# Grouped attention values, joined gate and up rows, and moved split and router steps in a hybrid encoder layer

## The chip, the cores and the metric

One core of one Trainium2 chip runs the whole layer as one program. The metric is device time in microseconds; the median of three runs before the change is 1883.89 us (1882.89 to 1885.06). The engines are named as the profile names them: PE multiplies matrices (PEld loads its weights), DVE, ACT and POOL do elementwise work, SP issues most transfers.

## What is computed

The layer mixes tokens (Fourier, neighbourhood attention and memory attention, gated and projected by `w_out`), normalises, and then sends each of 1024 tokens to 2 of 64 experts.

```python
proj = x @ w_in                                   # Fourier | q k v of the neighbourhood | memory q
br_na  = neighbourhood_attention(q_na, k_na, v_na, rpb) @ w_na_o
merged = gates[0] * br_f + gates[1] * br_na + gates[2] * br_mem
h = layer_norm(ALPHA * x + merged @ w_out)
# hierarchical_moe(h): one group of 8 by argmax, then the top 2 experts in it
yb = (jax.nn.silu(xb @ w_eg[e]) * (xb @ w_eu[e])) @ w_ed[e]
x = layer_norm(ALPHA * h + moe)
```

Everything is float32. An expert has a gate and an up matrix (1024 x 512 each) and a down matrix (512 x 1024), 2 MB apiece: 6.3 MB for each expert, 403 MB for all 64. An expert's tokens fill 64 slots.

## The kernel before

The first half (class `Dense`) is a chain of stages: the Fourier branch, neighbourhood attention (`na`), memory attention (`mem_attn`), `merge`, and the output projection with the router (`out_proj`). Large products are made in three products of rounded halves (a high and a low part made by `split`, L150: ACT copies, DVE subtracts). The input projections and gates are "jobs" of 48 matmuls of 128x512 each (L201); `adv(n)` puts n of them between the steps of the attention stages, so that PE always has something to do. A planner orders each engine's instructions by a simulated timeline; `keep_in_program_order` (also called `pin`) fixes the place of an instruction among the pinned ones of its engine.

**Neighbourhood attention.** Work goes by units (head pair `hp`, column block `j`, half of the rows `hf`, head of the pair `a`): `scores`, softmax, then one unit later `turned` (three transposes, L583). After the last of the four units of one (hp, j), `values` (L586, L593) issues eight products. Each is float32, which the trace shows as two matmul instructions, so a call is 16 instructions and there are 16 calls. Products for head a = 0 write the partitions 0 to 63 of a bank and those for a = 1 the partitions 64 to 127, and the program issues them in turn: a = 0, a = 1. They are not pinned.

**Merge.** For d = 0 to 7 two products of 24 matmuls each (L167) are made from weights that come through the raw tile `gr` (three buffers) and are split into `gh` and `gl`. In d = 1 to 4 `halves` (L710) sends two of the eight parts of `w_out` through the same three buffers: four transfers and four splits for each d. `w_out`'s halves stand in four 16 KB tiles `blk` of the pool WO.

**Output projection.** Eight tiles of 128 tokens, 48 matmuls each (L931), all pinned. Between the matmuls, at the places that the table `AT` (L783) lists, stand steps of earlier tiles: "t" transposes, "l" logits, "p" and "b" the middle and last part of `Moe.route`. "p" (L1132, L1133) counts with a table M that DVE has just made (L1126). `sums` (L807, L811) is put into the first tile once. `more()` issues the next weight transfer from SP: at tiles 0, 1, 2, 3 and 7, two more in `after(7)`, and then two from POOL behind the last tile (L1669).

**Experts.** `load` (L1324) brings 192 blocks of 2 MB (gate, up, down) into nine 16 KB-wide tiles: three in B1, two in Mg, four in WO; Mg and WO come free when `merge`'s and `out_proj`'s data have been used. A row, that is the bytes of one partition in one transfer, has 16 KB; the last expert is sent in four pieces a block (4 KB rows). For each expert `up` issues 8 pairs of products (gate to partitions 0 to 63, L1293; up to 64 to 127, L1294), `down` 4 pairs (L1315, L1316). `ahead` issues as many further loads as buffers come free. The transfers' waits for a free buffer stand on SP.

Of the kernel before, what the change touches and what calls it, by code (L numbers as in the profile page):

```python
# [5 lines left out]
F32 = mybir.dt.float32  # L6
FR = mybir.dt.float32r
# [8 lines left out]
D = 1024  # L16
T = 1024
NK = D // 128
# [110 lines left out]
class Dense:  # L129
# [116 lines left out]
    def start(s, pool):  # L246
# [22 lines left out]
        for j in range(2):  # L269
            s.wt[j] = [pool.tile([128, NK, 128], FR, name=n, bufs=2) for n in ("wh", "wl")]  # L270

# [273 lines left out]
    def na(s, fill):  # L545
# [39 lines left out]

        def values(u):  # L586
            hp, j, _, _ = u
            K = 4 * KCOLS[s.ORDER[j]][1]
            if j % 2 == 0:
                s.po = s.bank("o")  # L590
            for g, i, c in ((1, 1, slice(0, 2)), (0, 0, slice(0, 1)), (3, 0, slice(1, 2)), (2, 2, slice(0, 2))):
                for a in range(2):
                    nc.tensor.matmul(s.po[64 * a:64 * a + 64, j % 2 * 256 + c.start * 128:j % 2 * 256 + c.stop * 128],  # L593
                                     s.V[:K, j, g, hp * 128 + 64 * a:hp * 128 + 64 * a + 64],
                                     pts[a][:K, i, c].rearrange("p h f -> p (h f)"), start=g == 1, stop=g == 2)
            if j == 1:
# [10 lines left out]
        units = [(hp, j, hf, a) for hp in range(4) for j in range(4) for hf in range(2) for a in range(2)]  # L607
        old = None
        for i in range(len(units) + 1):
            u = units[i] if i < len(units) else None  # L610
            if u and u[1:] == (0, 0, 0):
                hp = u[0]
                if hp == 0:
                    s.finish("v3")
                s.finish(f"q{hp}")
                s.finish(f"k{hp}")
                s.adv(16)
                if hp == 0:
                    biases(0, "m")
                biases(hp, "e")  # L620
            if u and u[1:] == (2, 0, 0) and u[0] < 3:
                biases(u[0] + 1, "m")
            if u:
                sc = scores(u)
            s.adv(fill // 2)
            if old:
                turned(*old)
                s.adv(fill - fill // 2)
                if old[0][2:] == (1, 1):
                    values(old[0])  # L630
            old = (u, sc)

# [63 lines left out]
    def merge(s, W, pool, On, WO):  # L696
# [57 lines left out]

        blk = lambda: WO.tile([128, 4 * D], F32, name="blk", bufs=4)
        t = blk()
        raw = [t[:, k * D:(k + 1) * D] for k in range(4)]
# [6 lines left out]
        for d in range(8):  # L764
            get("s1", d, s.g_dram[8:])
            if d < 7:
                weights(0, d + 1)
                mem(d + 1)
                parts(0, d + 1)
            if d < 6:  # L770
                weights(1, d + 2)
                parts(1, d + 2)
            for k in range(2 * d - 2, 2 * d) if 0 < d < 5 else ():
                if k % 4 == 0:
                    s.wo.append([blk().bitcast(FR) for _ in range(2)])
                c = slice(k % 4 * D, (k % 4 + 1) * D)
                halves(*(t[:, c] for t in s.wo[-1]), A["w_out"][:, k])
            product(0, d)
            add_na(d)
        ps.release()  # L780


    AT = ((((11, "t", 1), (17, "l", 1)), ((11, "t", 0), (14, "p", 1), (17, "l", 0), (22, "b", 1))),  # L783
          (((11, "t", 1), (17, "l", 1)), ((21, "t", 0), (22, "p", 1)), ((6, "l", 0), (12, "t", 0), (16, "b", 1), (21, "l", 0))))

    def out_proj(s, P, P0, ps, lg, h_dram, done, more):
# [60 lines left out]
        def after(t, pl):  # L847
# [13 lines left out]
            if t == 7:  # L861
                for _ in range(2):
                    more()
            d = nc.gpsimd.dma_start(h_dram[t * 128:(t + 1) * 128], xts[t])
# [187 lines left out]
def moe_layout(i):  # L1052
    a = {}
    for n, k in (("w_exp_gate", 8), ("w_exp_up", 8), ("w_exp_down", 4)):
        w = np.asarray(i[n])[0]
        a[n] = np.ascontiguousarray(w.reshape(NE, k, 128, w.shape[2]).transpose(0, 2, 1, 3)).reshape(NE, 128, 4096)
    r = np.arange(128)
# [16 lines left out]
class Moe:  # L1074
# [210 lines left out]

    def up(s, ws, xT, mp, ps, nb, pin=lambda i: i):

        nc = s.nc
        wg, wu = ([w.rearrange("p (k f) -> p k f", f=512)[:, k] for w in ws[i] for k in range(w.shape[1] // 512)] for i in range(2))
        pg = ps.tile([128, 512], F32, name="pg")  # L1290
# [18 lines left out]

    def down(s, ws, hT, ps, bank="pd", pin=lambda i: i):  # L1310
        nc = s.nc
        wd = [w.rearrange("p (k f) -> p k f", f=1024)[:, k] for w in ws[2] for k in range(w.shape[1] // 1024)]
        pd = ps.tile([128, 512], F32, name=bank)
# [10 lines left out]
    def load(s, i, pool, bufs, eng=None):  # L1324

        e, k = s.ORDER[i]
        w = pool.tile([128, 4096], F32, name="blk", bufs=bufs)
        m = 1 if i < 3 * NE - 3 else 4
        for j in range(m):
            c = slice(j * 4096 // m, (j + 1) * 4096 // m)  # L1330
            d = (eng or s.nc.sync).dma_start(w[:, c], s.A[("w_exp_gate", "w_exp_up", "w_exp_down")[k]][e, :, c])
        return w, d

    def experts(s, w, more):
# [138 lines left out]

        def weights(e, k):
            return [w[s.ORDER.index((e, k))]]

        def up(e):
            c = slice(e % 2 * 64, e % 2 * 64 + 64)
            return s.up([weights(e, k) for k in range(2)], [xts[e // 2, i][:, j, c] for i in range(2) for j in range(4)], mp, ps, 1, pin)

        def ahead(n):
            while len(w) < min(3 * NE, n):
                d = more()
                if len(w) > 3 * NE - 6:
                    pin(d)

        for e in range(NE + 1):
# [3 lines left out]
            if e < NE:  # L1493
                gu = up(e)
                ahead(3 * e + 10)
            if e == 0:
# [10 lines left out]
            if e and e != NE - 1:  # L1507
                if e == NE:
                    last = half(FR)[:, :GR], mp.tile([128, 512], FR, name="gu"), half(FR)
                pd = s.down([None, None, weights(e - 1, 2)], hT, ps, "pd" if e < NE else "pg", pin)  # L1510
                ahead(3 * e + 11)
                new = accumulate(e - 1, pd)
# [15 lines left out]
            if e == NE - 2:  # L1528
                add(*accumulate(e, s.down([None, None, weights(e, 2)], hT, ps, pin=pin)))
        ps.release()  # L1530
# [3 lines left out]
    def slow(s, norm):  # L1534
# [5 lines left out]
        with tc.If(n > 0):  # L1540
# [15 lines left out]
            with tc.For_i(0, n, 1):  # L1556
# [21 lines left out]
                with tc.For_i(0, NE, 1) as e:  # L1578
                    c = nc.values_load(remi[0:1, bass.ds(e, 1)], min_val=-16 * SL, max_val=T)
                    with tc.If(c > 0):  # L1580
# [6 lines left out]
                        ws = []  # L1587
                        for nm in ("w_exp_gate", "w_exp_up", "w_exp_down"):
                            w = mp.tile([128, 4096], F32, name="o" + nm)
                            nc.sync.dma_start(w, A[nm][bass.ds(e, 1)].rearrange("o p f -> (o p) f"))  # L1590
                            ws.append([w])
                        pd = s.down(ws, s.act(s.up(ws, s.transposed(xg, mp, ps, 1), mp, ps, 1), mp, ps, 1), ps)
                        y = mp.tile([128, 512], F32, name="oy")
# [40 lines left out]
def build(tc, A):  # L1634
# [23 lines left out]

    pools = [(B1, 3)] * 3 + [(d.Mg, 2)] * 2 + [(d.WO, 4)] * 4

    def more(eng=None):
        i = len(w)
        t, ins = m.load(i, *pools[i % len(pools)], eng=eng)
        w.append(t)
        return ins
    d.out_proj(P, P0, ps, m.lg, h_dram, route, more)
    m.indices(P, *tabs)
    for _ in range(2):
        tc.keep_in_program_order(more(nc.gpsimd))  # L1669
    m.fetch(0)  # L1670
# [28 lines left out]
```

## Time and profile before

| | us |
|---|---|
| median of 3 runs | 1883.89 |
| the profiled execution | 1888.03 |
| its span, first to last instruction | 1886.3 |
| dense stages, to the last matmul of the output projection | 908 |
| experts, from there | 978 |

A profile comes from one execution. Where the rows give times such as 399.71, they are microseconds from the span's start. A matmul's record is longer than the distance to the next one, since matmuls overlap in the array; so what a matmul costs is read here from the start of one to the start of the next.

### The profile page before, as it was taken

To read this page: it belongs to the slowest core of one execution; us is meant where nothing else is said; L and a number is where in the kernel's file an instruction comes from. 1 tells how busy PE (TensorE), PEld (TensorE's weight loads), DVE (VectorE), ACT (ScalarE), POOL (GpSimd) and SP (SyncE) were. 2 spreads that over 40 slices of the span, in tenths; PEclk is the share of its full clock that TensorE was granted. 3 is DMA by queue.
4 is the path that set the end of the run, shared out by engine and by line. 5 is a ranking of instruction groups with operands and counts; after the bars stand their busy time and mean duration, and the time that the engine had idled before them with its cause. 6 is when DMAs were issued, how large, how long until landed. Compare 5 with 4: busy or idle time off the path is not lost. (4 is left out here: it accounts for less than half of the span.)

```text
span 1886.3 us, 23170 instructions
## 1 busy us (share of the span) xinstructions
PE 1819.5 (96%) x9290; PEld 1116.2 (59%) x9291; DVE 678.4 (36%) x1610; ACT 445.8 (24%) x819; POOL 126.5 (7%) x108
## 2 busy tenths in 40 slices
PE   8999999999999999999899999999999999999995
PEld 6988888777777777777644444434343343344331
DVE  5343234453442537677612222112221121212212
ACT  4332123343333432111211212112120121111211
POOL 1000100101200000000100101001010010100100
PEclk9999999999999999999999999999999999999998
DMA  7254513323233237652799999999999999999993
GB/s 280 71 196 152 195 45 98 99 95 110 93 95 128 79 140 248 217 201 101 306 411 426 427 426 427 428 418 427 426 426 428 426 427 425 422 427 427 427 426 156
DMA packets 77991, 527.31 MB, mean 280 GB/s; under 512 B 10447, under 2 KB 12383, under 8 KB 53176
## 3 DMA queue, kind: packets, MB, share of 16 engines
q1 hardware_dynamic: 55448, 469.31, 61.1%
q10 hardware_dynamic: 16352, 35.07, 5.5%
q0 software_dynamic: 6080, 21.42, 3.0%
q8 instruction: 74, 1.21, 0.3%
q14 instruction: 37, 0.30, 0.1%
HBM read 493.59 MB, written 32.51 MB: 279 GB/s over the span
## 5 line engine op out<-in xcount | busy, mean ns | idle before, releaser
L1294 PE MATMUL pg<-blk,xT 128*64 128x512 f32 x1024 | 456.6, 599 | 24.2 <-DMA blk<-in_w_exp_up 24.1
L1293 PE MATMUL pg<-blk,xT 128*64 128x512 f32 x1024 | 464.2, 601 | 0.3 <-ACT xT L1383 0.3
L1416 DVE SCALAR_TENSOR_TENSOR yl<-pd,wcol,yh 128x512 fp32r<-128x512 f32 x63 | 47.3, 751 | 667.7 <-ACT yh L1415 667.7
L201 PE MATMUL mm<-xl,wh 128*128 128x512 f32 x672 | 266.2, 396 | 0.0
L201 PE MATMUL mm<-xh,wh 128*128 128x512 f32 x672 | 265.1, 394 | 0.0
L201 PE MATMUL mm<-xh,wl 128*128 128x512 f32 x672 | 264.3, 394 | 0.0
L1294 PEld LDWEIGHTS pg<-blk,xT 128*64 128x64 f32 x1024 | 135.7, 137 | 202.5 <-issue 146.2
L1316 PE MATMUL pd<-blk,hTe 128*64 128x512 f32 x504 | 226.6, 592 | 0.0
L1315 PE MATMUL pd<-blk,hTe 128*64 128x512 f32 x504 | 226.6, 592 | 0.0
L1293 PEld LDWEIGHTS pg<-blk,xT 128*64 128x64 f32 x1024 | 132.7, 137 | 139.0 <-issue 134.7
L1296 ACT ACTIVATE gu<-pg 128x512 f32<-128x512 f32 x64 | 38.2, 597 | 567.1 <-PE pg L1294 567.1
L201 PEld LDWEIGHTS mm<-xh,wh 128*128 128x128 f32 x672 | 126.4, 188 | 25.5 <-issue 0.9
L201 PEld LDWEIGHTS mm<-xl,wh 128*128 128x128 f32 x672 | 126.4, 188 | 25.3 <-issue 1.6
L201 PEld LDWEIGHTS mm<-xh,wl 128*128 128x128 f32 x672 | 126.4, 188 | 25.0 <-issue 0.9
L1316 PEld LDWEIGHTS pd<-blk,hTe 128*64 128x64 f32 x504 | 69.0, 137 | 82.8 <-issue 82.8
L1315 PEld LDWEIGHTS pd<-blk,hTe 128*64 128x64 f32 x504 | 69.0, 137 | 61.2 <-issue 60.8
L152 DVE TENSOR_TENSOR wl<-wr,wh 128x1024 fp32r<-128x1024 f32 (+2 forms) x54 | 64.3, 1193 | 112.7 <-ACT wh L151 112.2
L1415 ACT ACTIVATE yh<-pd,wcol 128x512 fp32r<-128x512 f32 x63 | 43.3, 687 | 176.6 <-PE pd L1316 176.6
L151 ACT ACTIVATE wh<-wr 128x1024 fp32r<-128x1024 f32 (+2 forms) x54 | 55.5, 1028 | 109.0 <-PE mm L201 105.7
L931 PE MATMUL mm<-blk,mh 128*128 128x512 f32 (+1 forms) x272 | 70.9, 394 | 0.8 <-ACT mh L151 0.8
L1368 PE MATMUL tp<-sel,hh 128*128 128x128 f32 x248 | 70.1, 283 | 0.8 <-DVE xT L1371 0.8
L1369 PE MATMUL tp<-sel,hl 128*128 128x128 f32 x248 | 68.2, 275 | 0.0
(371 smaller groups left out, 2451.7 us busy)
## 6 DMA issues: line engine op xcount, KB each, us to landing
blk<-in_w_exp_up SPq DMA_DIRECT2D x63, 2048.0 KB, 37.0
blk<-in_w_exp_gate SPq DMA_DIRECT2D x62, 2048.0 KB, 32.9
blk<-in_w_exp_down SPq DMA_DIRECT2D x62, 2048.0 KB, 39.1
wr<-in_w_g SPq DMA_DIRECT2D x24, 512.0 KB, 3.7
g_dram<-gt ACTq DMA_DIRECT2D x48, 256.0 KB, 2.1
s<-g_dram SPq DMA_DIRECT2D x32, 256.0 KB, 3.9
be<-in_rpb_e ACTq DMA_DIRECT2D x8, 576.0 KB, 5.8
gt<-g_dram SPq DMA_DIRECT2D x8, 512.0 KB, 4.6
```

What stands on the lines that cost most here:

```text
L151: s.nc.scalar.activation(hi, src, AF.Copy)
L152: s.nc.vector.tensor_tensor(out=lo, in0=src, in1=hi.bitcast(F32), op=OP.subtract)
L201: s.nc.tensor.matmul(p[:, :width], st[:, k], x[:, k, c], start=k == 0 and pi == 0, stop=k == NK - 1 and pi == 2)
L931: pin(nc.tensor.matmul(p, (mh, mh, ml)[i][:, k], wo[c.start // 512][i % 2][:, at:at + w], start=j == 0, stop=j == m - 1))
L1293: pin(nc.tensor.matmul(pg[0:64], l, wg[k], start=k == 0, stop=k == 7))
L1294: pin(nc.tensor.matmul(pg[64:128], l, wu[k], start=k == 0, stop=k == 7))
L1315: pin(nc.tensor.matmul(pd[0:64], hT[:, f], wd[f][:, 0:512], start=f == 0, stop=f == 3))
L1316: pin(nc.tensor.matmul(pd[64:128], hT[:, f], wd[f][:, 512:1024], start=f == 0, stop=f == 3))
L1368: pin(nc.tensor.matmul(tp[:, j], hh[:, c], o[:, 0], start=True, stop=False))
L1369: pin(nc.tensor.matmul(tp[:, j], hl[:, c], o[:, 0], start=False, stop=False))
L1415: nc.scalar.activation(yh, pd, AF.Copy, scale=s.wcol[:, e:e + 1])
L1416: nc.vector.scalar_tensor_tensor(yl, pd, s.wcol[:, e:e + 1], yh.bitcast(F32), op0=OP.mult, op1=OP.subtract)
```

## The change

- `values` is pinned, and a call is issued one unit later: behind the scores of the next unit but one, ahead of the next `turned`.
- Gate and up of an expert are interleaved on the host into one array, and come in one transfer of 4 MB with rows of 32 KB. B1, WO and Mg hold the same bytes, now as three 32 KB tiles for gate and up and three 16 KB tiles for down. `w_out`'s high and low halves share one 32 KB tile.
- `more()` is called at tiles 0, 1, 3 and 7, once in `after(7)` and once from POOL.
- `halves` sends one part of `w_out` in each of d = 0 to 7.
- In `AT`, "p" goes from place 14 to 18 and "b" from place 22 of the tile to place 3 of the next one; `sums` goes from place 10 to 19.
- At the start the split weights of the second job go to the pool W.

```diff
-            s.wt[j] = [pool.tile([128, NK, 128], FR, name=n, bufs=2) for n in ("wh", "wl")]
+            s.wt[j] = [(pool, s.W)[j].tile([128, NK, 128], FR, name=n, bufs=1 + j) for n in ("wh", "wl")]
...
-        def values(u):
+        def values(u, pts):
...
-                    nc.tensor.matmul(s.po[64 * a:64 * a + 64, j % 2 * 256 + c.start * 128:j % 2 * 256 + c.stop * 128],
-                                     s.V[:K, j, g, hp * 128 + 64 * a:hp * 128 + 64 * a + 64],
-                                     pts[a][:K, i, c].rearrange("p h f -> p (h f)"), start=g == 1, stop=g == 2)
+                    s.tc.keep_in_program_order(nc.tensor.matmul(
+                        s.po[64 * a:64 * a + 64, j % 2 * 256 + c.start * 128:j % 2 * 256 + c.stop * 128],
+                        s.V[:K, j, g, hp * 128 + 64 * a:hp * 128 + 64 * a + 64],
+                        pts[a][:K, i, c].rearrange("p h f -> p (h f)"), start=g == 1, stop=g == 2))
...
             s.adv(fill // 2)
+            if due:
+                values(*due)
+                due = ()
             if old:
                 turned(*old)
                 s.adv(fill - fill // 2)
                 if old[0][2:] == (1, 1):
-                    values(old[0])
-            old = (u, sc)
+                    due = old[0], dict(pts)
+            old = (u, sc) if u else None
...
-            for k in range(2 * d - 2, 2 * d) if 0 < d < 5 else ():
-                if k % 4 == 0:
-                    s.wo.append([blk().bitcast(FR) for _ in range(2)])
-                c = slice(k % 4 * D, (k % 4 + 1) * D)
-                halves(*(t[:, c] for t in s.wo[-1]), A["w_out"][:, k])
+            if d % 4 == 0:
+                t = blk().bitcast(FR)
+                s.wo.append([t[:, :4 * D], t[:, 4 * D:]])
+            c = slice(d % 4 * D, (d % 4 + 1) * D)
+            halves(*(t[:, c] for t in s.wo[-1]), A["w_out"][:, d])
...
-    AT = ((((11, "t", 1), (17, "l", 1)), ((11, "t", 0), (14, "p", 1), (17, "l", 0), (22, "b", 1))),
-          (((11, "t", 1), (17, "l", 1)), ((21, "t", 0), (22, "p", 1)), ((6, "l", 0), (12, "t", 0), (16, "b", 1), (21, "l", 0))))
+    AT = ((((3, "b", 2), (11, "t", 1), (17, "l", 1)), ((11, "t", 0), (17, "l", 0), (18, "p", 1))),
+          (((3, "b", 2), (11, "t", 1), (17, "l", 1)), ((21, "t", 0), (22, "p", 1)), ((6, "l", 0), (12, "t", 0), (16, "b", 1), (21, "l", 0))))
...
-            if t in (0, 1, 2, 3, 7):
+            if t in (0, 1, 3, 7):
...
-                    if (t, n, j) == (0, 1, 10):
+                    if (t, n, j) == (0, 1, 19):
...
-    ORDER = [(e - k // 2, k) for e in range(NE - 1) for k in range(3) if 0 <= e - k // 2]
-    ORDER += [(NE - 2, 2)] + [(NE - 1, k) for k in range(3)]
+    ORDER = [("gu", 0), ("d", 0), ("d", 1), ("d", 2), ("gu", 1), ("gu", 2), ("gu", 3)]
+    ORDER += [x for e in range(4, NE - 1) for x in (("gu", e), ("d", e - 1))] + [("d", NE - 2), ("gu", NE - 1), ("d", NE - 1)]
...
                 gu = up(e)
-                ahead(3 * e + 10)
+                if e < NE - 4:
+                    upto("gu", e + 3)
...
-    pools = [(B1, 3)] * 3 + [(d.Mg, 2)] * 2 + [(d.WO, 4)] * 4
+    pools = {"gu": [(B1, "gu", 1)] + [(d.WO, "blk", 2)] * 2, "d": [(B1, "dn", 1)] + [(d.Mg, "blk", 2)] * 2}
...
-    for _ in range(2):
-        tc.keep_in_program_order(more(nc.gpsimd))
+    tc.keep_in_program_order(more(nc.gpsimd))
```

## Rows read from the trace of the kernel before

**Rows 1.** Stretches: us, busy PE (x), PEld, DVE, ACT, POOL, clock, DMA share, GB/s.

```profile
320.00:591.00 271.00, 271.00 (x1402) 210.80 (x1401) 123.31 (x357) 99.83 (x216) 28.20 (x13) 1.00 0.30 96
...
950.00:1835.00 885.00, 861.02 (x4380) 359.76 (x4376) 195.61 (x402) 148.72 (x238) 65.57 (x40) 1.00 1.01 426
```

**Rows 2.** Who waited for whom on PE: total us, times, longest us.

```profile
PE pg L1294 <- DMA blk<-in_w_exp_up: 24.1, 34, 2.6
PE t L1133 <- DVE M L1126: 5.6, 7, 2.5
...
PE t L811 <- DVE mh L809: 1.4, 1, 1.4
```

**Rows 3.** Timeline, PE, one usual call of values: start, length, what, count.

```profile
399.38 0.40 PE L201 MATMUL mm<-xh,wh 128*128 128x512 f32 x1
399.71 0.65 PE L593 MATMUL o<-pt,V 128*64 128x256 f32 x2
400.29 0.55 PE L583 MATMUL t<-ident,sc 128*128 128x128 f32 x3
...
401.26 0.39 PE L201 MATMUL mm<-xh,wl 128*128 128x512 f32 x1
401.49 0.39 PE L201 MATMUL mm<-xh,wh 128*128 128x512 f32 x1
401.81 1.51 PE L593 MATMUL o<-pt,V 128*64 128x256 f32 x14
403.25 0.55 PE L583 MATMUL t<-ident,sc 128*128 128x128 f32 x3
```

**Rows 4.** Timeline, PE, a call at the end of a head pair.

```profile
380.47 0.65 PE L593 MATMUL o<-pt,V 96*64 96x256 f32 x2
381.04 0.44 PE L563 MATMUL s<-KH,QS 128*128 128x384 f32 x1
381.42 0.43 PE L593 MATMUL o<-pt,V 96*64 96x128 f32 x2
381.78 0.45 PE L563 MATMUL s<-KL,QS 128*128 128x384 f32 x1
382.15 1.08 PE L593 MATMUL o<-pt,V 96*64 96x128 f32 x10
383.17 0.45 PE L563 MATMUL s<-KH,QS 128*128 128x384 f32 x1
```

**Rows 5.** Timeline, one pair of expert 0's gate and up products.

```profile
924.86 0.59 PE L1293 MATMUL pg<-blk,xT 128*64 128x512 f32 x1
924.86 0.59 PE L1294 MATMUL pg<-blk,xT 128*64 128x512 f32 x1
```

**Rows 6.** Stretches of the merge, columns as in group 1.

```profile
736.00:748.00 12.00, 9.18 (x37) 7.10 (x36) 8.61 (x17) 3.67 (x6) 0.00 (x0) 0.89 0.79 245
748.00:760.00 12.00, 12.00 (x45) 9.53 (x44) 8.67 (x17) 3.68 (x6) 0.00 (x0) 0.82 0.77 243
760.00:772.00 12.00, 12.00 (x53) 9.68 (x52) 6.17 (x12) 1.88 (x3) 0.00 (x0) 1.00 0.45 147
```

**Rows 7.** Timeline of the merge: PE's wait; in brackets the idle time before it.

```profile
746.12 2.07 PE L167 MATMUL pg<-Om,gh 128*128 128x512 f32 x4 [2.82 <-ACT gh L151]
```

**Rows 8.** Timeline of the output projection: step "p" of one tile.

```profile
874.07 0.21 PE L1132 MATMUL t<-R,ones 128*128 128x72 bf16 x1
...
874.80 0.19 PE L1133 MATMUL t<-M,tri 128*128 128x72 bf16 x1 [0.53 <-DVE M L1126]
```

**Rows 9.** Timeline: issue of the last loads ahead of the experts.

```profile
900.44 30.95 SPq L1331 DMA_DIRECT2D blk<-in_w_exp_up  x2
...
919.79 0.62 POOL L1331 DMA_DIRECT2D blk<-in_w_exp_down  x1
```

**Rows 10.** Page: the packets of all transfers.

```profile
DMA packets 77991, 527.31 MB, mean 280 GB/s; under 512 B 10447, under 2 KB 12383, under 8 KB 53176
```

**Rows 11.** A stretch in which the last expert's 4 KB rows move, columns as in group 1.

```profile
1845.00:1850.00 5.00, 4.71 (x24) 1.68 (x24) 1.40 (x3) 0.97 (x2) 0.00 (x0) 1.00 0.99 388
```

More of the change, by code (lines that the diff above doesn't have):

```diff
@@ L607, in na @@
         units = [(hp, j, hf, a) for hp in range(4) for j in range(4) for hf in range(2) for a in range(2)]
-        old = None
-        for i in range(len(units) + 1):
+        old, due = None, ()
+        for i in range(len(units) + 2):
             u = units[i] if i < len(units) else None
@@ L753, in merge @@
         parts(1, 1)
-        blk = lambda: WO.tile([128, 4 * D], F32, name="blk", bufs=4)
-        t = blk()
+        blk = lambda: WO.tile([128, 8 * D], F32, name="blk", bufs=2)
+        t = blk()[:, :4 * D]
         raw = [t[:, k * D:(k + 1) * D] for k in range(4)]
@@ L861, in after @@
             if t == 7:
-                for _ in range(2):
-                    more()
+                more()
             d = nc.gpsimd.dma_start(h_dram[t * 128:(t + 1) * 128], xts[t])
@@ L1053, in moe_layout @@
     a = {}
-    for n, k in (("w_exp_gate", 8), ("w_exp_up", 8), ("w_exp_down", 4)):
-        w = np.asarray(i[n])[0]
-        a[n] = np.ascontiguousarray(w.reshape(NE, k, 128, w.shape[2]).transpose(0, 2, 1, 3)).reshape(NE, 128, 4096)
+    g, u = (np.asarray(i[n])[0].reshape(NE, 8, 128, 512) for n in ("w_exp_gate", "w_exp_up"))
+    a["w_exp_gu"] = np.ascontiguousarray(np.stack([g, u], 3).transpose(0, 2, 1, 3, 4)).reshape(NE, 128, 8192)
+    w = np.asarray(i["w_exp_down"])[0]
+    a["w_exp_down"] = np.ascontiguousarray(w.reshape(NE, 4, 128, D).transpose(0, 2, 1, 3)).reshape(NE, 128, 4096)
     r = np.arange(128)
@@ L1284, in transposed, with up @@
         return [xT[:, h, j] for h in range(2) for j in range(4)]
-    def up(s, ws, xT, mp, ps, nb, pin=lambda i: i):
+    def up(s, w, xT, mp, ps, nb, pin=lambda i: i):
         nc = s.nc
-        wg, wu = ([w.rearrange("p (k f) -> p k f", f=512)[:, k] for w in ws[i] for k in range(w.shape[1] // 512)] for i in range(2))
+        wg, wu = ([w.rearrange("p (k i f) -> p k i f", i=2, f=512)[:, k, i] for k in range(8)] for i in range(2))
         pg = ps.tile([128, 512], F32, name="pg")
@@ L1308, in act, with down @@
         return hT
-    def down(s, ws, hT, ps, bank="pd", pin=lambda i: i):
+    def down(s, w, hT, ps, bank="pd", pin=lambda i: i):
         nc = s.nc
-        wd = [w.rearrange("p (k f) -> p k f", f=1024)[:, k] for w in ws[2] for k in range(w.shape[1] // 1024)]
+        wd = [w.rearrange("p (k f) -> p k f", f=1024)[:, k] for k in range(4)]
         pd = ps.tile([128, 512], F32, name=bank)
@@ L1317, in down, with load @@
         return pd
-    ORDER = [(e - k // 2, k) for e in range(NE - 1) for k in range(3) if 0 <= e - k // 2]
-    ORDER += [(NE - 2, 2)] + [(NE - 1, k) for k in range(3)]
[L1324 to L1328, printed above, removed]
+    ORDER = [("gu", 0), ("d", 0), ("d", 1), ("d", 2), ("gu", 1), ("gu", 2), ("gu", 3)]
+    ORDER += [x for e in range(4, NE - 1) for x in (("gu", e), ("d", e - 1))] + [("d", NE - 2), ("gu", NE - 1), ("d", NE - 1)]
+    def load(s, i, pools, eng=None):
+        k, e = s.ORDER[i]
+        pool, name, bufs = pools[k][e % 3]
+        n = 8192 if k == "gu" else 4096
+        w = pool.tile([128, n], F32, name=name, bufs=bufs)
+        m = 1 if e < NE - 1 else 4
         for j in range(m):
-            c = slice(j * 4096 // m, (j + 1) * 4096 // m)
-            d = (eng or s.nc.sync).dma_start(w[:, c], s.A[("w_exp_gate", "w_exp_up", "w_exp_down")[k]][e, :, c])
+            c = slice(j * n // m, (j + 1) * n // m)
+            d = (eng or s.nc.sync).dma_start(w[:, c], s.A["w_exp_gu" if k == "gu" else "w_exp_down"][e, :, c])
+            if i > len(s.ORDER) - 5:
+                s.tc.keep_in_program_order(d)
         return w, d
@@ L1472, in add, with weights, upto @@
                     sc.append(d)
-        def weights(e, k):
-            return [w[s.ORDER.index((e, k))]]
+        def weights(k, e):
+            return w[s.ORDER.index((k, e))]
         def up(e):
             c = slice(e % 2 * 64, e % 2 * 64 + 64)
[L1479 to L1485, printed above, removed]
+            return s.up(weights("gu", e), [xts[e // 2, i][:, j, c] for i in range(2) for j in range(4)], mp, ps, 1, pin)
+        def upto(k, e):
+            while (k, e) in s.ORDER[len(w):]:
+                more()
         for e in range(NE + 1):
@@ L1509, in experts @@
                     last = half(FR)[:, :GR], mp.tile([128, 512], FR, name="gu"), half(FR)
-                pd = s.down([None, None, weights(e - 1, 2)], hT, ps, "pd" if e < NE else "pg", pin)
-                ahead(3 * e + 11)
+                pd = s.down(weights("d", e - 1), hT, ps, "pd" if e < NE else "pg", pin)
+                upto("d", e + 2)
+                if e == NE - 4:
+                    upto("gu", NE - 1)
                 new = accumulate(e - 1, pd)
@@ L1528, in experts @@
             if e == NE - 2:
-                add(*accumulate(e, s.down([None, None, weights(e, 2)], hT, ps, pin=pin)))
+                add(*accumulate(e, s.down(weights("d", e), hT, ps, pin=pin)))
         ps.release()
@@ L1587, in slow @@
                         ws = []
-                        for nm in ("w_exp_gate", "w_exp_up", "w_exp_down"):
-                            w = mp.tile([128, 4096], F32, name="o" + nm)
+                        for nm in ("w_exp_gu", "w_exp_down"):
+                            w = mp.tile([128, A[nm].shape[2]], F32, name="o" + nm)
                             nc.sync.dma_start(w, A[nm][bass.ds(e, 1)].rearrange("o p f -> (o p) f"))
-                            ws.append([w])
-                        pd = s.down(ws, s.act(s.up(ws, s.transposed(xg, mp, ps, 1), mp, ps, 1), mp, ps, 1), ps)
+                            ws.append(w)
+                        pd = s.down(ws[1], s.act(s.up(ws[0], s.transposed(xg, mp, ps, 1), mp, ps, 1), mp, ps, 1), ps)
                         y = mp.tile([128, 512], F32, name="oy")
@@ L1657, in build @@
     w = []
-    pools = [(B1, 3)] * 3 + [(d.Mg, 2)] * 2 + [(d.WO, 4)] * 4
+    pools = {"gu": [(B1, "gu", 1)] + [(d.WO, "blk", 2)] * 2, "d": [(B1, "dn", 1)] + [(d.Mg, "blk", 2)] * 2}
     def more(eng=None):
-        i = len(w)
-        t, ins = m.load(i, *pools[i % len(pools)], eng=eng)
+        t, ins = m.load(len(w), pools, eng=eng)
         w.append(t)
@@ L1667, in build @@
     m.indices(P, *tabs)
-    for _ in range(2):
-        tc.keep_in_program_order(more(nc.gpsimd))
+    tc.keep_in_program_order(more(nc.gpsimd))
     m.fetch(0)
```

## The prediction

> **What bounds the kernel now.** I read the stretches first. Between 950 and 1835 us the DMA engines are busy all the time and move 426 GB/s [rows 1], and PE's largest wait there is for an expert's weights [rows 2]: the experts are bound by the weight stream, at 6.29 MB / 426 GB/s = 14.8 us an expert. The stretch from 320 to 591 is the opposite: PE is busy throughout, the DMA share is 0.30 [rows 1], and no PE wait of that stretch stands among the waits. A view of busy time alone would end here. But records of matmuls overlap, so what an instruction costs is the distance between starts, and these show where PE spends its full stretch badly (values), idles (merge), or waits for DVE (router).
>
> The two halves meet at one point. Nine buffers of 2 MB are filled ahead of the experts; SP's last free ones wait for the last tile of the output projection, and POOL's follow behind it [rows 9]. From then on the stream runs without a gap. So a microsecond taken out of any dense stage starts the stream a microsecond earlier and counts in full; in the expert half only the stream's rate counts.
>
> **Values.** There are 16 calls of 16 instructions, in 38 runs, the first at 327.24 and the last at 588.96. Thirteen calls look as [rows 3]: head 0's first product goes alone as 2 instructions, 14 follow later. The pair costs 400.29 - 399.71 = 0.58 us, plus the step into it: 399.71 - 399.38 = 0.33 where a job's matmul takes 401.49 - 401.26 = 0.23, so 0.10. The 14 cost 403.25 - 401.81 = 1.44 and 0.09 to enter: 2.21 in all. The pair gives the price of 256 columns, (0.58 less the switches) / 2, about 0.215, and so 0.11 for 128. One after the other the 14 would take 6 x 0.215 + 8 x 0.11 = 2.2, but they take 1.44: the two heads use different columns of the array and run side by side. Head 1 has all of its 8 among the 14, 4 x 0.215 + 4 x 0.11 = 1.30 and switches, which is the 1.44. Head 0's missing two therefore fit beside it for nothing, and a call held together costs 1.44 + 0.09 = 1.53. Saved: 0.68 x 13 = 8.8 us. Pinning alternate halves does pair them: gate and up, pinned the same way, start in the same 10 ns [rows 5].
>
> Three calls, at the ends of head pairs, are cut in four. The one in [rows 4] has an early pair as above (0.68), and then 383.17 - 380.47 = 2.70, in which two L563 stand that remain (384 columns each, some 0.2 apiece): about 3.0 against 1.53, so 1.5 x 3 = 4.6. Together **13.4 us**. Issuing the call a unit later adds no instruction; it keeps the transposed tiles a unit longer, and they have four buffers for two live pairs. PE is full in this stretch, so nothing hides the gain. Who is late next: memory attention's own steps, which the job matmuls cover as before. Bounds: 8.8 (only the usual calls mend) to 14.5 (the transposes behind a removed run lose their 0.05 of switching too).
>
> **Merge.** At 746.12 PE had idled 2.82 us for a split of weights on ACT [rows 7]. ACT, in order, had first to split `w_out` parts that were still landing through the same three raw buffers: six users of them for each d in d = 1 to 4, four after the change, and two more users at d = 0 and d = 5 to 7. The wait also costs clock. 12 us hold 53 matmuls at full clock, but 37 and then 45 around the wait, where the granted clock is 0.89 and 0.82 [rows 6], partly at the lower of its two levels, 1.2 GHz. Lost: 24 x 12 / 53 = 5.4 us. With a third fewer users at d = 3 I take **5.0**. Bounds: 5.4, and 0 if the wait only moves. SP is moved past nothing else here: the two transfers of d = 7 stand ahead of the router tables, which are first used in `sums`, beyond the first tile's first half.
>
> **Output projection.** Step "p" issues L1132 at 874.07 and L1133 at 874.80, waiting for M [rows 8]; the two alone take some 0.06, so 0.67 is lost. Seven such waits are listed, the longest, 2.5, at the last tile [rows 2], which keeps its place: 6 x 0.67 = 4.0. Four matmuls and eight logits later (4 x 0.23 and more) M is there. "b" moves as a whole into the next tile; what it needs on DVE was ready at its old place, and it makes the same switches. `sums` waits 1.4 [rows 2]; nine matmuls later (9 x 0.23 = 2.1) it does not. The next tile's split, which needs the buffer that `sums` reads, comes some 0.3 later and is not due before the tile ends. Together **5.4**; bounds 3 and 5.6.
>
> **Weights.** Ahead of the experts the bytes are the same at each point: 6 MB at the first tiles, 2 at tile 3, 2 at tile 7, 4 behind `after(7)`, 4 from POOL. One thing is later: SP's 4 MB now wait for both halves of `w_out`'s first tile, until 900.44 [rows 9]; 4.2 MB at 426 GB/s are over by 911, ahead of POOL's at 919.79, so this costs nothing. In the experts the order of bytes and the reuse of buffers (after three experts) are unchanged, and `up` waited for the second of its two blocks before as now.
>
> The rate: a 16 KB row on one of 16 engines takes 16384 x 16 / 426 = 615 ns [rows 1]; a 4 KB row, at 388 / 0.99 = 392 GB/s, 167 ns [rows 11]. A line through both has 37.3 ns for a KB and 18 ns for a row. 24064 of the 24815 packets of 8 KB or more [rows 10] are 188 blocks x 128 rows, so a row went as one packet. If one of 32 KB does, each engine saves 18 ns on 8 rows for some 60 experts: 8.6 us; if it is cut, 0. The short pieces end more often, which makes 18 ns too high; I take **4**.
>
> What speaks against long rows: POOL's fetches of the first group's tokens share the engines with SP's stream. The Trainium skill (DMA: Bandwidth & Descriptors, Queues, rings and completion order) says that an engine drains a whole packet of one queue before it turns to another. By that rule a fetched row waits behind 32 KB instead of 16 KB. Without the page: 8 rows an engine, up to 0.6 us later each, less than 5 us, on a stream which at that time has three blocks (14.8 us) queued; I count nothing, and 3 in the range.
>
> The weights of the second job at the start: the same splits into another pool, nothing; a late split would cost some 2 once.
>
> **Sum.** 13.4 + 5.0 + 5.4 + 4.0 = 27.8 us. The profiled execution took 1888.0, span and what lies around it, and would take 1860.2; the median of the runs is 4.1 lower, so 1883.9 - 27.8 = **1856**. With all upper bounds 1883.9 - 34.1 = 1850, and with all lower ones (8.8 + 0 + 3 + 0 less 3) 1875; several of the lower ones together are unlikely.
>
> **Rivals.**
> - The merge's wait only moves, to d = 0 or to d = 5 to 7, and long rows bring nothing. For it: ACT is in order, and `w_out` parts are still split ahead of weights. Against: fewer users of three buffers. 1883.9 - 18.8 = 1865. Chance 0.17.
> - The change doesn't do what it says: pinned in a chain, the two heads no longer run side by side. A call would take 8 x 0.215 + 8 x 0.11 + 0.19 = 2.8; 16 of them 44.7 against 13 x 2.21 + 3 x 3.0 = 37.7 now, 7.0 lost instead of 13.4 won: 1856 + 20.4 = 1876. Against it: [rows 5]. Chance 0.05.
> - Slower: rows of 32 KB move more slowly, in the whole expert stage. 60 experts x 4.19 MB = 252 MB take 591 us now; the 23.8 us won elsewhere are lost once these rows fall below 252 / 614.8 = 410 GB/s. At the 392 of [rows 11] they would take 643, 52 more: 1883.9 - 23.8 + 52 = 1912. Nothing in the trace moves rows over 16 KB, so it can't be excluded, but the line of rows only rises. The same page (Latency and other measured facts) reports copies that slow down as the pitch between partitions' rows grows in powers of two, first at 512 KB and more; here it grows from 16 to 32 KB, and no row shows a loss at 16. Chance 0.05.
> - Little happens (within 4 us), as another resource starts the stream late: 0.03.
>
> **How the numbers follow.** The forecast, 1850 to 1861, has 0.70. The range must also take the first rival, so 1848 to 1869 (0.70 and most of 0.17, less what lies outside on either side). About 0.2% is what a measurement of this kernel can tell from no change. Faster by more: 0.70 + 0.17 + 0.05 = 0.92; within: 0.03; slower: 0.05.
>
> **What would show it.** Values: 16 runs of 16 instructions and about 1.45 us to the next start, or else runs of 2.6. Merge: no stretch of 12 us below 50 matmuls between 700 and 780. Projection: the wait for M once instead of seven times, none before `sums`. Stream: GB/s between 950 and 1800 of 427 to 432; a packet count lower by some 8000 if rows stay whole. Wrong would be a rate under 426, a PE wait that is new in the merge or in memory attention, or a stream that does not start some 24 us earlier.

## The result, and the profile after

The changed kernel takes 1874.9 us (median of nine runs, 1868.65 to 1879.81) against 1884.81 of the kernel before (nine runs): a ratio of 0.9946, 95% interval 0.9929 to 0.9962. It is 9.9 us faster, where 27.8 were forecast. Its profiled execution took 1872.23 us, span 1870.4.

That profile and the one of before (1888.03) are 15.9 us apart, the medians 9.9: the profile of before caught one of the longer executions of its kernel, this one a shorter one. A second profile of the same changed kernel, taken in the experiments, had a span of 1880.7. So no difference of two single profiles is trusted below unless other profiles repeat it. In the first pair of profiles the first product of expert 0 moves from 923.95 to 913.47, 10.5 us earlier, where some 24 had been named as the sign.

First the stretches of after, with the columns of [rows 1] (us, busy PE (x), PEld, DVE, ACT, POOL, clock, DMA share, GB/s). The first and last line answer to [rows 1], the two between them to [rows 6]:

```profile
320.00:591.00 271.00, 271.00 (x1405) 210.57 (x1404) 121.55 (x357) 100.61 (x216) 27.97 (x14) 1.00 0.31 97
736.00:748.00 12.00, 12.00 (x54) 9.72 (x53) 9.39 (x17) 2.70 (x5) 0.00 (x0) 1.00 0.74 232
748.00:760.00 12.00, 12.00 (x53) 9.75 (x52) 8.02 (x15) 2.53 (x4) 0.00 (x0) 1.00 0.74 238
950.00:1835.00 885.00, 842.18 (x4408) 376.46 (x4406) 198.21 (x405) 149.74 (x240) 65.67 (x40) 0.98 1.00 428
```

The stretch of the values holds 1405 matmuls instead of 1402: almost nothing was gained there. The merge has its 53 matmuls in 12 us again. The stream moves 428 GB/s instead of 426, in packets of two sizes (page of after, the line of [rows 10]):

```profile
DMA packets 68342, 527.30 MB, mean 282 GB/s; under 512 B 9375, under 2 KB 11311, under 8 KB 51080
```

A 32 KB row went as one packet. Then who waited for whom on PE, as in [rows 2]:

```profile
PE pg L1297 <- DMA blk<-in_w_exp_gu: 28.3, 18, 2.8
...
PE mm L934 <- ACT mh L151: 2.6, 1, 2.6
PE pg L167 <- ACT gh L151: 2.5, 2, 1.8
PE t L1137 <- DVE M L1130: 2.5, 1, 2.5
```

The wait for M stands once instead of seven times and the wait of `sums` is gone, as forecast. New is the first product of the output projection (L934): 2.6 us for the split of its left operand. The timeline of PE shows the values:

```profile
400.11 0.39 PE L201 MATMUL mm<-xl,wh 128*128 128x512 f32 x1
400.42 1.52 PE L593 MATMUL o<-pt,V 128*64 128x256 f32 x16
401.88 0.87 PE L583 MATMUL t<-ident,sc 128*128 128x128 f32 x6
...
411.75 0.39 PE L201 MATMUL mm<-xl,wh 128*128 128x512 f32 x1
412.07 0.65 PE L593 MATMUL o<-pt,V 128*64 128x256 f32 x2
412.65 0.53 PE L583 MATMUL t<-ident,sc 128*96 128x128 f32 x3
...
414.07 1.51 PE L593 MATMUL o<-pt,V 128*64 128x256 f32 x14
415.52 0.53 PE L583 MATMUL t<-ident,sc 128*96 128x128 f32 x3
```

One call of 16 stands together, at 400.42, and costs 401.88 - 400.42 = 1.46 as forecast. The other fifteen are split as in [rows 3 and 4]: 37 runs instead of 38. Pinned and issued later, the first pair of matmul instructions, head 0's, still goes alone.

### The profile page after: what moved, and what is told of

Its sections match the earlier page's. It is cut to its first block, busy times and chain, and to the rows that moved or that the text cites. A ratio compares the mean times of both kernels' runs of the same rounds, so it can differ in the third digit from the quotient of the medians.

```text
span 1870.4 us, 23048 instructions
## 1 busy us (share of the span) xinstructions
PE 1790.5 (96%) x9290; PEld 1128.8 (60%) x9291; DVE 674.6 (36%) x1610; ACT 447.1 (24%) x819; POOL 125.8 (7%) x107
## 5 line engine op out<-in xcount | busy, mean ns | idle before, releaser
L1297 PE MATMUL pg<-blk,xT 128*64 128x512 f32 x672 | 307.7, 612 | 28.3 <-DMA blk<-in_w_exp_gu 28.3
L1298 PE MATMUL pg<-blk,xT 128*64 128x512 f32 x672 | 308.2, 613 | 0.0
L1297 PEld LDWEIGHTS pg<-blk,xT 128*64 128x64 f32 x672 | 91.1, 141 | 215.6 <-issue 209.6
L1297 PE MATMUL pg<-gu,xT 128*64 128x512 f32 x352 | 159.7, 607 | 14.2 <-DMA gu<-in_w_exp_gu 14.2
L1298 PE MATMUL pg<-gu,xT 128*64 128x512 f32 x352 | 159.9, 608 | 0.0
L1320 PE MATMUL pd<-blk,hTe 128*64 128x512 f32 x336 | 151.1, 592 | 0.0
L1319 PE MATMUL pd<-blk,hTe 128*64 128x512 f32 x336 | 151.1, 592 | 0.0
L1297 PEld LDWEIGHTS pg<-gu,xT 128*64 128x64 f32 x352 | 47.4, 140 | 111.1 <-issue 106.8
L1319 PEld LDWEIGHTS pd<-blk,hTe 128*64 128x64 f32 x336 | 45.9, 137 | 91.3 <-issue 90.9
L1298 PEld LDWEIGHTS pg<-blk,xT 128*64 128x64 f32 x672 | 91.1, 141 | 0.0
L1320 PE MATMUL pd<-dn,hTe 128*64 128x512 f32 x168 | 75.5, 592 | 0.0
```

Of the source, the lines that this page charges most:

```text
L1297: pin(nc.tensor.matmul(pg[0:64], l, wg[k], start=k == 0, stop=k == 7))
L1298: pin(nc.tensor.matmul(pg[64:128], l, wu[k], start=k == 0, stop=k == 7))
L1319: pin(nc.tensor.matmul(pd[0:64], hT[:, f], wd[f][:, 0:512], start=f == 0, stop=f == 3))
L1320: pin(nc.tensor.matmul(pd[64:128], hT[:, f], wd[f][:, 512:1024], start=f == 0, stop=f == 3))
```

## The experiments

All ratios are against the kernel before, timed on the same chip in turn with the kernel named.

**Head 1 first.** In the changed kernel, one edit of the order within a call:

```diff
-                for a in range(2):
+                for a in (1, 0):
```

> The changed kernel with one edit: in a call of values the product of head 1 is issued ahead of that of head 0. Head 1's transposed tile is made last, so the first product of a call is no longer ready before the rest. Theory: pinning fixed only the order of the pinned products among themselves, and the planner still put the one product that was ready early ahead of jobs and transposes; with head 1 first 13 of 16 calls stand together as 16 instructions, 1.45 us to the next start instead of 0.58 + 1.45, and the three at the ends of head pairs stand in three runs instead of four. 12 calls x 0.67 + 3 x 0.67 = 10 us are saved against the changed kernel, the first product of expert 0 starts at 903.5 instead of 913.5, and the time is 1865. Rival: PE was going to wait for head 1's tile anyway, or the jobs that stood between are missing later; then memory attention ends less than 4 us earlier and the time is 1871 to 1875.

It took 1866.14 us, ratio 0.9891 (0.9876 to 0.9906). The timeline of this kernel:

```profile
328.36 0.30 PE L563 MATMUL s<-KL,QS 128*128 128x288 f32 x1
328.59 1.52 PE L593 MATMUL o<-pt,V 128*64 128x256 f32 x16
330.04 0.87 PE L583 MATMUL t<-ident,sc 128*128 128x128 f32 x6
```

There are 22 runs: 13 calls of 16, and the three at the ends of head pairs in three pieces. The last job matmul stands at 676.67 instead of 687.07 and 687.39 (the two profiles of the changed kernel), 10.4 to 10.7 us earlier. The theory holds for the calls, and up to that point nothing was given back. The first product of expert 0 started at 905.61, not at the 903.5 expected, but 7.9 and 12.2 us earlier than in those two profiles (913.47 and 917.79): merge and the clock behind it, which vary from execution to execution (see below), lie between.

**Head 1 first alone,** in the kernel before, without pins and without the later issue:

```diff
-                for a in range(2):
+                for a in (1, 0):
                     nc.tensor.matmul(s.po[64 * a:64 * a + 64, ...
```

> The kernel before with one edit: in a call of values the product of head 1 is issued ahead of that of head 0; nothing is pinned, nothing issued later, all else as before. Theory: what holds a call together is the order of its first two products alone, so 13 of 16 calls stand as 16 instructions here too, and 10 to 11 us are saved: ratio 0.9943, first product of expert 0 at 913 instead of 924. Rival: the 10.5 us that this edit saved in the changed kernel also needed the pins or the later issue; then the runs are split in another way and less than half of it is saved, ratio 0.997 or above.

1875.2 us, ratio 0.9933 (0.9919 to 0.9946): 12 us from one line, as much as the whole change or more (9.9, and 8.0 in a second measurement below; the intervals overlap). PE's order has the same 22 runs, 13 of them whole calls:

```profile
400.60 0.39 PE L201 MATMUL mm<-xl,wh 128*128 128x512 f32 x1
400.92 1.52 PE L593 MATMUL o<-pt,V 128*64 128x256 f32 x16
402.37 0.55 PE L583 MATMUL t<-ident,sc 128*128 128x128 f32 x3
```

The last job matmul moves from 688.23 to 678.40, 9.8 us, and the first product of expert 0 from 923.95 to 911.50, of which 2.9 are a shorter merge (see below). So the pins and the later issue together did next to nothing (one call of sixteen in the changed kernel), and what is taken from the dense half does count in full.

**Rows.** Four kernels. First the changed kernel once more, then the joined rows without the rest (but with their order of loads and the pool of the second job's weights), then the rest with rows of 16 KB:

> The changed kernel once more, unchanged, as the partner of the other three. Its first profiled execution took 1872.2 us and its nine times have a median of 1874.9, and the profiled execution of the kernel before took 1888.0 at a median of 1884.8: the two profiles differ by 15.9 us, the medians by 9.9. If 32 KB rows make the stream faster by what the two profiles show (30 to 370 MB of weights in 809.4 us against 814.0), this second profile shows 809 again. If the stream's time differs from execution to execution whatever the rows, it shows something else, between 806 and 817, while the dense stages end where they ended (first product of expert 0 at 913.5, within 1 us).

> The changed kernel with values, the split of w_out, and the router's steps put back as they were before; what is left of the change is the joined 32 KB rows with their order of loads, and the pool of the second job's weights. If 32 KB rows bring 4 to 5 us, the time is 1880 against 1884.8 of the kernel before (ratio 0.9976). If they bring nothing, it is within 1.5 us of the kernel before. The first product of expert 0 starts at 924 in both cases.

```diff
-        m = 1 if e < NE - 1 else 4
+        m = (2 if k == "gu" else 1) if e < NE - 1 else 4
```

> The changed kernel with the joined gate and up block fetched by two transfers of 2 MB with rows of 16 KB instead of one of 4 MB with rows of 32 KB; all else is as in the changed kernel. If a row costs 18 ns beside its bytes, as I worked out before, or about 10, as the first two profiles say (4.6 us), the time is 4 to 9 us above the changed kernel: 1879 to 1884, and 30 to 370 MB of weights take 814. If row length makes no difference and the two profiles differed by chance, the median is within 1.5 us of the changed kernel's in this same job.

| | ratio (95%) | 340 MB of weights, us |
|---|---|---|
| changed kernel, first time | 0.9946 (0.9929 to 0.9962) | 809.3 |
| changed kernel again | 0.9949 (0.9933 to 0.9965) | 809.7 |
| 32 KB rows alone | 0.9976 (0.9966 to 0.9986) | 810.0 |
| 16 KB rows, rest as changed | 0.9999 (0.9989 to 1.001) | 814.0 |
| kernel before | 1 | 814.0 |

The last column is the time between the starts of the packets (of 16 KB and more) that pass 30 and 370 MB; which early packets are counted moves it by some 0.5 us. It is the same within about 1 us in every execution for one length of row, so the first row-length theory holds and chance is out: 4 to 5 us in 340 MB. The medians of the packets say the same, 1216 ns for 32 KB against 2 x 614 = 1228 for two of 16 KB. 32 KB rows alone gain 0.24%, 4.5 us.

The dense half did not repeat as expected: in the second profile of the changed kernel the first expert started at 917.8, not within 1 us of 913.5. It has 18 products around merge at half clock (the lower of the two levels, 1.2 GHz: 0.427 us from start to start instead of 0.233), the first profile has none.

The 16 KB kernel lost 9 to 10 us against the changed kernel, though, not 4 to 5. Its POOL queue shows a side effect of the edit (timeline; in brackets the idle time before):

```profile
904.36 1.06 POOL L1336 DMA_DIRECT2D blk<-in_w_exp_gu  x2 [9.22 <-PE mm L934]
909.53 0.54 POOL L867 DMA_DIRECT2D h_dram<-xt  x1 [4.12 <-DVE ix L1119]
922.79 1.08 POOL L1179 DMA_INDIRECT xt<-h_dram,six  x1 [12.72 <-DMA h_dram<-xt]
```

Only the second half of POOL's transfer was pinned. The first went ahead of the last store of h, the store waited among 4 MB of weights, and the first expert's tokens with it. Mended by pinning both halves:

```diff
-            if i > len(s.ORDER) - 5:
+            if i > len(s.ORDER) - 5 or eng and j < m - 1:
```

> The changed kernel with 16 KB rows for gate and up, two transfers of 2 MB as in the earlier kernel of that kind, but with both halves of the transfer that POOL issues held behind the last store of h. In the earlier one the first half went ahead of that store, the store was late and so was the first expert (928.3 instead of 913.5 to 917.8). Theory: 32 KB rows save 12 ns in 1228 and nothing else of weight; the first expert starts at 913 to 918, 340 MB take 814 us, and the median is 4 to 5 us above the changed kernel's 1874.9 to 1878.6: 1880 to 1883. Rival: the short rows also let the fetched token rows through sooner, so the stream has no gap behind expert 0 and half of that comes back: 1877 to 1880.

1877.39 us, ratio 0.9942 (0.9928 to 0.9955), 814.0 us for 340 MB. The first expert started at 919.4 in its profile, a little behind the 913 to 918 expected. The stream is 4 us slower, and yet the end is no later than that of the changed kernel: the ratios put it 1 us below, 3 either way by their intervals, which leaves no room for 4 to 5 above. The theory falls; something in the changed kernel takes back what its long rows win. The second profile of the changed kernel shows one such loss, in a stretch where the stream should be full (columns as above):

```profile
931.00:937.00 6.00, 4.27 (x20) 1.20 (x18) 1.77 (x3) 2.72 (x3) 1.08 (x1) 1.00 0.88 373
937.00:943.00 6.00, 4.92 (x30) 2.60 (x26) 2.66 (x6) 2.50 (x4) 0.98 (x1) 1.00 0.31 93
```

and its waits between 917 and 946, on ACT, DVE and SP's queue:

```profile
ACT hh L1351 <- DMA xt<-h_dram,hidx: 7.4, 1, 7.4
...
DVE hl L1353 <- ACT hh L1351: 5.8, 1, 5.8
...
DVE h L1354 <- ACT h L1352: 4.1, 1, 4.1
...
SPq L1547 <- DVE nblk L1273: 16.9, 1, 16.9
```

POOL's fetched rows land late. ACT and DVE, which split them, wait in order, and on DVE the four steps that make `nblk` stand behind that split although they could have run at 928. SP waits for `nblk` and issues nothing; for 5.2 us no weight packet is in motion (the expectation below counts the same hole as 6.4, and that of the kernel with head 1 first, 2.9 by this count, as 4.1). In the first profile SP waited 8.8, and there was no hole. The last two rows of that late fetch moved at 929.74 and 931.11, 1.37 us apart, which is the length of one 32 KB packet and one row (1216 and 159 ns): what the prediction cited from the Trainium skill (DMA: Bandwidth & Descriptors, Queues, rings and completion order), that an engine drains a whole packet before it turns to another queue, agrees with these two. Over all profiles the long rows did not make the fetch later, though: the split of the fetched rows began 10.6 to 15.1 us after the first expert in the five profiles with 32 KB rows and the old place of `nblk` (mean 12.0), and 10.7 to 12.6 in the three with 16 KB rows and an undisturbed start (mean 11.9).

**nblk first.** On the kernel with head 1 first: the split and the next fetch are issued behind `flags`, whose last four steps are pinned.

```diff
-        split(pin)
-        fetch(1)
...
                 s.flags(small, ps.tile([128, 512], F32, name="pd"))
+                split(pin)
+                fetch(1)
...
-        nc.vector.tensor_copy(s.nblk, mx[0:1])
+        pin(nc.vector.tensor_copy(s.nblk, mx[0:1]))
```

> The changed kernel with head 1 first, and with the four DVE steps that count the overfull experts (they end in nblk, for which SP waits) pinned ahead of the split of the first group's fetched tokens, not behind it. Theory: the split waits for the fetched rows, nblk stands behind it on DVE, SP behind nblk, and the weight stream ran dry for 4.1 us in the profile of the kernel with head 1 first alone (6.4 us in the second profile of the changed kernel, 0 in its first). With nblk ahead SP's wait for nblk ends within 12 us after the first product of expert 0, no gap over 1.5 us stands in the stream between 910 and 950, and the median falls by 2 to 5 us below the 1866 of head 1 first, to 1861 to 1864, with a smaller spread. Rival: SP's next transfers wait for their buffers, which PE is still reading, as long; then the median stays within 1.5 us of 1866.

1863.11 us, ratio 0.9876 (0.9861 to 0.9891). DVE's order is mended (timeline), the wait of SP is 7.0 us, and the stream has no hole, as in three of five profiles with the old order:

```profile
916.82 0.14 DVE L1274 CAST nblk<-g 1x1 int32<-1x1 f32 x1
916.89 1.20 DVE L1354 TENSOR_TENSOR hl<-xt,hh 128x1024 fp32r<-128x1024 f32 x1
```

`nblk` came 14.5 us after the first expert's start, not within 12: a step of the expert (L1312, waiting 2.93 for ACT) still stood between its four steps. The median fits the theory; its interval overlaps that of head 1 first alone, so the 3 us by themselves aren't shown.

**w_out earlier.** The new wait at the end of merge, in the timeline of the changed kernel:

```profile
765.69 0.33 SPq L718 DMA_DIRECT2D gr<-in_w_out  x1
766.37 0.80 SPq L732 DMA_DIRECT2D s<-g_dram  x2
...
776.02 1.95 SPq L732 DMA_DIRECT2D s<-g_dram  x3
778.66 0.69 DVE L737 SCALAR_TENSOR_TENSOR s<-s,pg 128x512 f32<-128x512 f32 x1 [1.04 <-DMA s<-g_dram]
779.38 0.39 PE L167 MATMUL pg<-On,gl 128*128 128x512 f32 x1
...
782.33 1.42 PE L934 MATMUL mm<-blk,mh 128*128 128x512 f32 x5 [2.57 <-ACT mh L151]
```

The last gate tiles are fetched from 776.02 on, 3.4 us ahead of the last merge product, where before it was 6.5 (781.53 and 787.99); DVE waits for them, and the split that PE waits for comes behind. SP had itself waited before 776.02, for a buffer that DVE frees (the longest of these waits, 3.7 us; SP's queue, 740 to 785):

```profile
SPq L732 <- DVE blk L746: 6.1, 8, 3.7
```

The last `w_out` transfer was issued at 765.69. So if these transfers delay the tiles, they do it through the chain of buffers and splits behind them. On the kernel with head 1 first:

```diff
-            halves(*(t[:, c] for t in s.wo[-1]), A["w_out"][:, d])
+            for k in ((0,), (1,), (2,), (3,), (4, 5), (6,), (7,), ())[d]:
...
+                halves(*(t[:, c] for t in s.wo[-1]), A["w_out"][:, k])
```

> The changed kernel with head 1 first, and with the eight parts of w_out at d = 0, 1, 2, 3, 4 (two), 5, 6, none at d = 7. Theory: the w_out transfers of d = 6 and 7 stand on SP ahead of the last gate tiles, DVE waits for these, and the first product of the output projection comes 3.0 to 4.9 us behind the last of merge instead of 1.2, with half clock behind it where the wait is over 4. Without a part at d = 7 that distance falls to 1.2 to 2, no product behind it runs at half clock, and 2 to 5 us are saved: 1861 to 1864. Rival: two parts at d = 4 bring back a wait inside merge and what is won at the end is lost there; the time stays within 1.5 us of 1866.

1863.27 us, ratio 0.9875 (0.9859 to 0.989). The distance behind merge is 1.92 us instead of 4.90 and no product runs at half clock behind it, as expected. But a new wait of 1.6 stands inside merge, and from the last job matmul to the output projection it takes 95.4 us against 96.2: part of the gain only moved. Nor does this pair show that the part at d = 7 was to blame: the kernel with nblk first has it too, and in its profile the distance is 1.66 and the stage 94.5. Of six profiles with that part it is the only one under 2.9; the three without it have 1.70 to 1.97.

**All four mends,** with "b" at place 6:

```diff
-    AT = ((((3, "b", 2), (11, "t", 1), ...
+    AT = ((((6, "b", 2), (11, "t", 1), ...
```

> The changed kernel with four edits together: head 1 first in values, nblk's four steps ahead of the split of fetched tokens, no part of w_out at d = 7 (two at d = 4), and step "b" at place 6 instead of 3 of the next tile. Theory: the four losses are separate and stand on the path that starts the weight stream, so their mends add up: head 1 first alone has a median of 1866.1; the distance behind merge falls by about 2 to 3 us (with the half clock behind it), nblk's gap, 3 us in that kernel's profile, goes, and the seven waits of "b" (0.25 us each, 1.75) go: 1858 to 1861, and the first expert starts at 900 to 902. Rival: the mends overlap, each only moves the wait on, as the two kernels with one mend both ended at 1863; then the time is 1862 to 1864.

> The kernel with all four mends, with gate and up in rows of 16 KB (two transfers of 2 MB). Theory: with nblk no longer behind the fetched tokens the long rows cost nothing, and their 12 ns a row are won in full: 4 to 5 us slower than the same kernel with 32 KB rows, 340 MB in 814 us against 809.7. Rival: row length makes no difference to the end, as the changed kernel with 16 KB rows, both halves pinned, had 0.9942 against 0.9946 and 0.9949; then both are within 1.5 us of each other.

1860.0 us (1858.33 to 1862.42), ratio 0.9866 (0.985 to 0.9883): 26 us ahead of the kernel before, the best of this study. The median and the first expert's start, 901.1, are what the theory forecast, but the interval, 1858 to 1864, takes in the rival as well, so that the losses were separate isn't shown by the time. By stages the mend of "b" shows plainly (113.5 us for the output projection against 115.4 in the kernel with `w_out` earlier); that of `w_out` doesn't (merge 95.25, and 94.50 with the old split in the kernel with nblk first). With 16 KB rows it takes 1864.63, ratio 0.9889 (0.9873 to 0.9906): 4.6 us more, and no time of the one kernel lies among those of the other. Here SP waits 4.1 and 3.6 us for `nblk`, no hole stands in either stream, and the long rows are worth what the packets say. Stretches of the two, 32 KB first, then 16 KB:

```profile
950.00:1800.00 850.00, 806.03 (x4230) 361.71 (x4226) 190.17 (x392) 143.65 (x230) 65.62 (x40) 0.98 1.01 428
```

```profile
950.00:1800.00 850.00, 799.43 (x4220) 344.19 (x4218) 190.16 (x392) 143.04 (x229) 65.56 (x40) 1.00 1.01 426
```

## Where the prediction was right and wrong

| term, us | forecast | the two profiles | over all profiles |
|---|---|---|---|
| values, to the last job matmul | 13.4 | 1.2 | 0.7 |
| merge | 5.0 | 5.7 | 2.5 |
| output projection | 5.4 | 3.9 | 2.3 (3.8 less half clock) |
| first expert to last gate product | 4.0 | 5.2 | 4.3 without a hole in the stream; with one, 1.9 and 6.2 less |

The last column sums to 9.8, and to 8.2 with the holes' share of 1.6 (see below); the two measurements of the changed kernel say 9.9 and 8.0.

**Values: the step that failed.** The prediction said "a call held together costs 1.44 + 0.09", and took holding together from the word pin, though a pin, as the section on the kernel says, fixes places among pinned instructions only. Jobs and transposes aren't pinned there, so the planner went on putting the first product, head 0's, ahead as soon as its tile was ready. The rival "the change doesn't do what it says" asked only whether the pairs would stop running side by side, and not whether the pins would do nothing; that would have been 1883.9 - 27.8 + 13.4 = 1869.5, the largest single correction. The bound was wrong with it: the range took values at 8.8 or more, so that the measured 1874.9 next to the 1875 of all lower bounds is chance. The price itself was right: by its own terms 13 calls and three runs less are 16 x 0.68 = 10.9, and 9.8 to 10.7 came.

**Merge: sized by one execution.** The kernel before took 100.93 us from the last job matmul to the output projection, with 20 products at half clock (0.427 us each instead of 0.233: the lower of the two levels, 1.2 GHz). Two other kernels with the same merge took 98.42 and 98.02 with none. Six profiles with the new split took 94.5 to 98.8, mean 96.7. The gain is 2.5, half of the 5.0. "SP is moved past nothing else here" was wrong: the transfers of d = 6 and 7 stand ahead of the last gate tiles, and a wait came back at the end of merge (1.7 to 5.0 us instead of 1.2), in four of six profiles with 9 to 13 products at half clock behind it. The first rival had said that the wait moves, and named d = 5 to 7. That these transfers cause it is argued from the order on SP; the runs without a part at d = 7 fit, but do not prove it.

**Output projection.** Six waits for M and that of `sums` went as priced: 4.2 and 1.5. But "what it needs on DVE was ready at its old place" does not hold for the new place. At 3 of the next tile DVE has the tile just ended to take over (L936), between the two tables S (L1170), and the last product of "b" waits for the second (timelines of the changed kernel, DVE then PE, and of the one with "b" at 6):

```profile
881.93 0.28 DVE L1170 TENSOR_SCALAR S<-rc,pos 128x128 bf16<-128x128 f32 x1
...
882.28 0.69 DVE L936 SCALAR_TENSOR_TENSOR xt<-mm,xt 128x512 f32<-128x512 f32 x1
882.89 0.28 DVE L1170 TENSOR_SCALAR S<-rc,pos 128x128 bf16<-128x128 f32 x1
...
882.84 0.23 PE L1162 MATMUL tg<-rg,Sg 128*128 128x80 bf16 x2
882.91 0.51 PE L1171 MATMUL tb<-rs,S 128*128 128x64 bf16 x2
883.26 0.48 PE L934 MATMUL mm<-blk,mh 128*128 128x512 f32 x1
```

```profile
871.52 0.23 PE L1163 MATMUL tg<-rg,Sg 128*128 128x80 bf16 x2
871.59 0.22 PE L1172 MATMUL tb<-rs,S 128*128 128x64 bf16 x2
871.65 0.71 PE L935 MATMUL mm<-blk,mh 128*128 128x512 f32 x2
```

883.26 - 882.91 = 0.35 against 0.06, in six tiles (the seventh "b" kept its place; the expectation above counted seven): 1.7 of the 5.7 went back. The stage took 119.2, then 115.3, and 113.5 with "b" at 6.

**Rows and gathers.** 4 us was right (4 to 5 in 340 MB; 12 ns a 32 KB row, not 18). The gathers' cost, counted at nothing because "three blocks are queued", was wrong in its reason: the stream lived not by the blocks queued at the start but by SP, which would refill the queue and waits behind the fetched rows (14.0 and 16.9 us in the two profiles with a hole, 8.3 to 10.7 in the six without). A hole stands in two of the five profiles of kernels with 32 KB rows and the old place of `nblk` (5.2 and 2.9 us), and in none of the three with 16 KB rows whose start was undisturbed. That is about 1.6 us on average over the five; the changed kernel with 16 KB rows should then still be some 3 us slower than with 32, and was not. The intervals, about 3 us either way, leave that open, and so the cause of this part.

**The rest** stands: the dense half counts in full, and the tail didn't change (26.0 and 25.7 us from the last gate product to the end).

## What to carry to other kernels

Before pricing what a pin does, ask which instructions it binds and which stay free, and ask why the planner placed an instruction early; here it was one operand ready too soon, and the order of two products was the mend. A queue that waits for a value waits for all that stands ahead of that value's steps on another in-order engine: move the few steps that release a transfer queue to the front (here tried, at most some 3 us, not shown by itself). And size a stall by several executions: the profile of before had 2.7 us more of it than its neighbours.

## What the runs showed of the hardware

The same wait of 2.2 us behind the last job matmul was followed by seven or eight products at half clock in five of twelve profiles and by none in seven. The two profiles of the changed kernel, the first and the second (columns as above):

```profile
684.00:696.00 12.00, 10.19 (x45) 7.97 (x44) 5.19 (x7) 6.14 (x8) 0.00 (x0) 1.00 0.64 224
```

```profile
684.00:696.00 12.00, 10.19 (x37) 7.75 (x36) 5.07 (x7) 6.13 (x8) 0.00 (x0) 0.86 0.60 215
```

With equal work and equal waits the granted clock is 1.00 in the one and 0.86 in the other, 45 matmuls against 37. Here the clock's part of the time was a matter of chance, not a sum to be added up.
